# The second mixer's gate projection as seven half-size products, its operand forms written over the activations' own quarters

## The chip, the cores and the metric

The kernel runs on one core of one Trainium2 chip. The metric is the device time of one execution in microseconds (us); lower is better. Five queues of instructions work side by side: TensorE (PE, the matmuls; its weight loads are listed apart as PEld), VectorE (DVE), ScalarE (ACT), GpSimd (POOL, here almost only the issuer of the DMAs that accumulate) and SyncE (SP, the issuer of most other DMAs).

## The reference, cut to what matters

A trunk of two layers on 512 tokens of width 1024, in float32. Layer 0 mixes with gated linear attention (GLA), layer 1 with a gated DeltaNet (GDN); after each comes a gated ConvFFN, and after every sublayer a layer norm. The change lies in layer 1's mixer:

```python
def gdn_mixer(x, w_in, conv_w, a_log, dt_bias, norm_w, w_out):
    proj = x @ w_in
    qkv, gate, beta_lin, a_lin = jnp.split(proj, [...], axis=-1)
    qkv = jax.nn.silu(causal_dwconv(qkv, conv_w))
    ...
    o = rms_norm(gdn_chunked(qc, kc, vc, beta, gc), norm_w)   # the recurrence, 4 chunks
    return (o * jax.nn.silu(gate)) @ w_out
```

The gate is `x` (512 x 1024) times a block of `w_in` (1024 x 1024).

## The kernel before, in words

**Number format.** Every large operand is kept as two float32r parts, a rounded high part and the rest (`xh`, `xl` for the activations, `wh`, `wl` for weights). A product of two such operands takes three matmuls: high by high, high by low, low by high. A weight item is one tile of 128 x 1024 (512 KB): ACT makes the high part by a cast, DVE the low part by a subtraction (`split_out`, line 716).

**Activations.** `xh` and `xl` hold x transposed: eight chunks of 128 features, each over 512 tokens. The quarters of x in what follows are (even or odd chunks) by (first or last 256 tokens): a11 is even and first, a21 even and last, a12 odd and first, a22 odd and last.

**Order of the work.** One Python planner writes all instructions. It takes weight items from `plan`, splits them `look` items ahead of use (`prefetch`), and keeps an estimated clock `clk`. Side work (the recurrence, the conversions) is written as generators, "tasks". After every six large matmuls `pump()` runs each task whose due time has come, as far as its next `yield`; a `yield 2.0` makes it due 2.0 us later on the planner's clock. `wait(name)` runs tasks without writing large matmuls until a flag is set. The program so written is then put in its final order for each engine by a scheduler that may move an instruction that is ready ahead of an earlier one that is not.

**The GDN mixer (`gdn`).** Its 24 head projections go through `fm_items`. Beside them tasks compute a decay, a Gram matrix per head and the inverse of a triangular system (`base`, `inverses`; line 1837 copies the last blocks of a pair of heads into `rm`, after which the flag `("rm", head)` is set). Then `chain(g)` runs the recurrence for heads 4g to 4g+3: four chunks, each of short float32 matmuls named ks, vn, kT, qs, s and o, with a DVE or ACT step between one and the next. Both chains run beside the gate projection.

**The gate projection before.** `gates` calls `x_tm` for each half of the 1024 output columns: 4 blocks of 128 tokens by 8 chunks by 3 matmuls of 128 x 512 (in the profile `tm<-wh,xh`, `tm<-wl,xh`, `tm<-wh,xl`), fed by eight weight items. Each finished block goes through a Silu on ACT (line 1284) into `sg`. `finish(hf)` waits for all four blocks of a half and for the norm of its heads (`r2`), multiplies (line 1972), and `split_y` transposes the result (`yT`) and splits it for the output projection (`out_proj`), whose residual `h` is read back by POOL's DMAs (`unspill`, line 978) and scaled on DVE (lines 987 and 988).

**The same idea elsewhere in this kernel.** The first mixer (`gla`) already computes its v and its gates by `gated`: a product of two 2 x 2 block matrices by seven products of half-size blocks instead of eight. Its forms of x (a11, a22, a12, w1 = a21 - a22, v2 = w1 - a11, v3 = a11 - a21, v4 = v2 + a12) are made by `x_forms` into tiles of their own, as xq (sums), xfh and xfl (parts). Its forms of the weights (`GATED`) are made in place: a tile (`gw`, or `raw`) is split, then another block of weights is added to it by an accumulating DMA on POOL's queue (line 462), then it is split again; one of the sums, t1 = b11 + b12, is made by a load and a DVE addition (line 454). The products accumulate in two pairs of PSUM banks; after each, `update` copies, adds or subtracts (lines 1220, 1228, 1235, 1238).

**Space.** `gdn` opens a pool of 45 slots of 128 x 512, and beside it `tt` and `m2`, two tiles of 128 x 1024 that `base` uses for the 32 x 32 inverses and no longer needs once they are written out (lines 1751 and 1752).

Of the kernel before, what the change touches and what calls it, by code (L numbers as in the profile page):

```python
# [15 lines left out]
P = 128  # L16
D = 1024
S = 512
# [16 lines left out]
GATED_NEW = {"b21": "b21", "b11": "b11", "t1": "b12", "b22": "b22"}  # L35
GATED_IN = {"b21": "b21", "b11": "b11", "t1": "b11", "b22": "b22", "t2": "b11", "t3": "b22", "t4": "b11"}
GATED_SUM = {"t1": "b22", "b22": "b12", "t2": "b21"}
PREPARE = (4.0, 16.0, 48.0, 68.0)
PREPARE_APART = (2.0, 4.5)
LN_EPS = 1e-5  # L40
# [36 lines left out]
class Trunk:  # L77
# [204 lines left out]
    def plan_gated(self, w, col):  # L282
        group = {"w": w, "col": col}
# [154 lines left out]
    def gated_load(self, group, name, i):  # L438


        if name not in GATED_NEW:
            return
        if name == "b11":
            t = self.mp.tile([P, 1024], F32, name=self.uid("gw"), tag="gw", bufs=2)
        else:
            t = self.rp.tile([P, 1024], F32, name=self.uid("raw"), tag="raw")
        self.nc.sync.dma_start(t.rearrange("p (j f) -> p j f", j=2), self.gated_rows(group, GATED_NEW[name], i))
        group[name, i] = t

    def issue_gated(self, group, name, i):  # L450
        nc = self.nc
        t = group[GATED_IN[name], i]
        if name == "t1":
            nc.vector.tensor_add(t, t, group.pop((name, i)))
            self.vec(1.24)
        self.held += 1
        wh = self.wp.tile([P, 1024], F32R, name=self.uid("wh"), tag="wh")
        wl = self.wp.tile([P, 1024], F32R, name=self.uid("wl"), tag="wl")
        self.split_out(wh, wl, t)
        self.vec(1.24)  # L460
        if name in GATED_SUM:
            nc.gpsimd.dma_start(t.rearrange("p (j f) -> p j f", j=2), self.gated_rows(group, GATED_SUM[name], i),
                                accum_op=ALU.add)
        if name in ("b21", "t3", "t4"):
            del group[GATED_IN[name], i]
        return [(wh[:, blk(j, S)], wl[:, blk(j, S)]) for j in range(2)]
# [101 lines left out]
    def tm_half(self, a, n, tail, done, slots=False, pieces=1):  # L568
# [19 lines left out]
        for tb in range(NTB):  # L588
            m = len(ps[tb])
            for piece in range(m):  # L590
# [9 lines left out]
    def x_tm(self, done):  # L600
        a = lambda c, tb: (self.xh[:, c, blk(tb)], self.xl[:, c, blk(tb)])
        self.tm_half(a, NC, 1, done)

    def out_proj(self, a, n, first, final, pieces=1):

# [543 lines left out]
    def x_forms(self, forms):  # L1149


        nc = self.nc
        pair = lambda t: t.rearrange("p (j i) -> p j i", j=2)

        def part(x, odd, tok, k):
            return x[:, 4 * k + odd:4 * k + odd + 3:2, tok:tok + 256]

        def full(odd, tok):
            ts = [self.slot("xq") for _ in range(2)]
            for k, t in enumerate(ts):  # L1160
                nc.vector.tensor_add(pair(t), *(part(x, odd, tok, k) for x in (self.xh, self.xl)))
            return ts

        def split(name, ts):
            forms[name] = []
            for t in ts:
                h, l = self.slot("xfh", F32R), self.slot("xfl", F32R)
                self.split_out(h, l, t)
                forms[name].append((h, l))
            self.set(("form", name), 2.0)  # L1170

        def both(a, b, op, out):
            for x, y, o in zip(a, b, out):
                nc.vector.tensor_tensor(o, x, y, op)

        for tb in range(NTB):
# [24 lines left out]
        split("v3", a)  # L1201

    def gated(self, forms, tag, done, last):


# [2 lines left out]
        top, high, right = ([None, None] for _ in range(3))  # L1208

        def operand(form, c, r):  # L1210
            if form in forms:
                cols = slice(c % 2 * 256 + r * P, c % 2 * 256 + r * P + P)
                return tuple(t[:, cols] for t in forms[form][c // 2])
            chunk = 2 * c + (form != "a11")
            tok = r * P + (256 if form == "a22" else 0)
            return self.xh[:, chunk, tok:tok + P], self.xl[:, chunk, tok:tok + P]
# [28 lines left out]
        for name, form, at in GATED:  # L1245
# [20 lines left out]
            else:  # L1266
                for i in (0, 2):
                    w = self.weight()
                    if name == "t4":
                        self.after = ()  # L1270
                    for r in range(2):
                        terms(i, w, r)
                        self.pump()
                    self.spend()
            if last:
                forms.pop(form, None)
        self.look = LOOKAHEAD

    def gates(self, sg):

        for hf in range(2):
            def done(tb, ps, hf=hf):
                t = self.slot("sg")
                self.nc.scalar.activation(t, ps, AF.Silu)
                sg[tb][hf] = t
                self.set(("sg", tb, hf), 2.0)

            self.x_tm(done)


    def gla_plan(self, w_in, w_out):
# [260 lines left out]
    def gdn_plan(self, w_in, w_out):  # L1552
        for hd in range(DH):
            if hd == HEADSTART:
                self.plan_pad([(w_in, 4096, 8, 0), (w_in, 4104, 8, H0)])
            self.plan_fm(w_in, 1024 + hd * P)
        for base in (2048, 0):
            for hd in range(DH):
                self.plan_fm(w_in, base + hd * P)
        for hf in range(2):  # L1560
            for cp in range(NC // 2):
                self.plan_tm(w_in, 2 * cp * P, 2, 3072 + hf * S)
        self.plan_out(w_out, 0, NC, TAIL)

    def gdn_consts(self, conv_w, a_log, dt_bias, norm_w):
# [24 lines left out]
    def gdn(self, li, g, b):  # L1590
# [370 lines left out]
                                           rr[:, hs4, :], ALU.mult, ALU.mult)  # L1961
            self.set(("r2", g), 2.5)

        def finish(hf):
            for tb in range(NTB):
                yield from self.until(("sg", tb, hf))
            yield from self.until(("r2", hf))
            for tb in range(NTB):
# [100 lines left out]
```

## Time and profile before

| | |
|---|---|
| three timed runs | 1221.22 to 1221.33 us, median 1221.23 |
| the profiled execution | 1221.98 us, its span 1220.2 us |
| PE, DVE, ACT, POOL busy | 99%, 74%, 50%, 13% of the span |
| granted TensorE clock | 1.000 |
| DMA | 149.41 MB, 122 GB/s |
| GDN mixer: head projections from, gate projection from, out projection from | 564.5, 724.7, 820.7 us |

Times in the lines below are us from the span's start; a mean is in ns. Matmuls overlap in the pipeline, so the busy time of one (some 390 ns for 512 columns) is longer than the distance from one to the next; the chain of waits gives the distance, as the length of a piece over its count of matmuls.

### The profile page before, as it was taken

Reading aid. Unit: us, or ns where it says so; the run is one execution under the profiler, and the core shown is the slowest. Engines: PE = TensorE matmul, PEld = TensorE weight load, DVE = VectorE, ACT = ScalarE, POOL = GpSimd, SP = SyncE. Lnnn points to the kernel's source line nnn. Section 1 sums busy time; section 2 is a strip of 40 time slices with the busy share of each in tenths; the row PEclk is TensorE's granted clock in tenths of the full one; section 3 lists DMA queues with packets and bytes.
Section 4 is the critical chain, followed back from the end, with each engine's and each line's share of the span. In section 5 each row is a group of like instructions: output and inputs, shape, how many; then the busy total and the mean of one; then the engine's idle time right before and its main releaser. Section 6 shows DMA issues by size and latency. Waiting matters only on the chain.

```text
span 1220.2 us, 17190 instructions
## 1 busy us (share of the span) xinstructions
PE 1213.6 (99%) x6501; PEld 1025.1 (84%) x6501; DVE 906.1 (74%) x1515; ACT 609.4 (50%) x1072; POOL 160.7 (13%) x203
## 2 busy tenths in 40 slices
PE   9999999999999999999999999999999999999998
PEld 8888888988888888889888888988988888888886
DVE  6989787787757675666789965688687757776667
ACT  5666663544434443454678555544644433443440
POOL 3030101601100110001242030200510100020000
PEclk9999999999999999999999999999999999999999
DMA  8384642536743554433444351335444853383311
GB/s 227 113 164 115 141 154 72 189 105 137 190 122 92 124 95 121 123 102 91 125 125 130 87 136 36 101 107 156 135 125 101 170 178 95 104 171 97 108 65 69
DMA packets 176275, 149.41 MB, mean 122 GB/s; under 512 B 16870, under 2 KB 140842, under 8 KB 176192
## 3 DMA queue, kind: packets, MB, share of 16 engines
q1 hardware_dynamic: 162464, 116.28, 32.2%
q0 software_dynamic: 12768, 31.37, 13.0%
q8 instruction: 51, 0.84, 0.3%
q10 hardware_dynamic: 960, 0.66, 0.2%
q14 instruction: 32, 0.26, 0.1%
HBM read 129.92 MB, written 5.78 MB: 111 GB/s over the span
## 4 chain that ended last, share of the span: by engine, by line
PE 97%; DMA 1%; ACT 1%; DVE 1%; SPq 0%; issue 0%; DVEq 0%
PE fm L213 54%; PE fold L213 19%; PE tm L213 15%; PE o L213 2%; PE xT L231 1%; DMA raw<-in_gla_w_in_dram 1%; PE pq L213 1%; PE pg L213 1%; PE vn L213 1%; PE yT L231 1%; PE V L213 0%; PE ds L213 0%; PE qs L213 0%; PE s L213 0%; PE ks L213 0%; DMA raw<-in_gdn_w_in_dram 0%
## 5 line engine op out<-in xcount | busy, mean ns | idle before, releaser
L213 PE MATMUL fm<-xh,wh 128*128 128x512 f32 (+2 forms) x1096 | 400.4, 368 | 0.7 <-ACT xh L716 0.7
L213 PE MATMUL fm<-xl,wh 128*128 128x512 f32 (+2 forms) x1096 | 398.5, 366 | 0.0
L213 PE MATMUL fm<-xh,wl 128*128 128x512 f32 (+1 forms) x1072 | 391.5, 367 | 0.2 <-DVE wl L716 0.2
L716 DVE TENSOR_TENSOR wl<-raw,wh 128x1024 fp32r<-128x1024 f32 (+1 forms) x158 | 195.4, 1239 | 151.7 <-ACT wh L716 151.3
L716 ACT CAST wh<-raw 128x1024 fp32r<-128x1024 f32 (+1 forms) x159 | 164.9, 1039 | 211.2 <-PE fm L213 135.5
L213 PEld LDWEIGHTS fm<-xh,wh 128*128 128x128 f32 (+1 forms) x1096 | 205.4, 188 | 34.1 <-ACT xh L716 0.9
L213 PEld LDWEIGHTS fm<-xl,wh 128*128 128x128 f32 (+1 forms) x1096 | 205.4, 188 | 32.6
L213 PEld LDWEIGHTS fm<-xh,wl 128*128 128x128 f32 x1072 | 201.2, 189 | 33.7 <-DVE wl L716 0.4
L1019 DVE SCALAR_TENSOR_TENSOR conv<-fm,ffn_cw,conv 128x511 f32<-128x511 f32 x112 | 83.5, 745 | 9.6 <-ACT conv L1017 7.9
L213 PE MATMUL fold<-wh,fh 128*128 128x512 f32 x224 | 87.6, 391 | 0.0
L213 PE MATMUL fold<-wh,fl 128*128 128x512 f32 x224 | 87.2, 389 | 0.0
L213 PE MATMUL fold<-wl,fh 128*128 128x512 f32 x224 | 87.1, 389 | 0.0
L716 ACT CAST wh<-b 128x1024 fp32r<-128x1024 f32 x48 | 50.0, 1054 | 74.2 <-PE fold L213 32.5
L716 DVE TENSOR_TENSOR wl<-b,wh 128x1024 fp32r<-128x1024 f32 x48 | 58.1, 1222 | 22.7 <-ACT wh L716 22.5
L412 POOL DMA_DIRECT2D b<-b x24 | 20.8, 902 | 357.2 <-DVE wl L716 306.7
L1037 ACT ACTIVATE conv<-conv 128x512 f32<-128x512 f32 x44 | 27.8, 632 | 63.3 <-DVE conv L1019 63.3
L1585 DVE SCALAR_TENSOR_TENSOR conv<-fm,gdn_cw,conv 128x511 f32<-128x511 f32 (+2 forms) x72 | 54.0, 788 | 5.1 <-ACT conv L1583 4.6
L213 PEld LDWEIGHTS fold<-wh,fh 128*128 128x128 f32 x224 | 42.0, 188 | 9.6 <-DVE h L1108 1.0
L213 PEld LDWEIGHTS fold<-wh,fl 128*128 128x128 f32 x224 | 42.0, 188 | 8.8
L213 PEld LDWEIGHTS fold<-wl,fh 128*128 128x128 f32 x224 | 42.1, 188 | 8.6
L1019 DVE SCALAR_TENSOR_TENSOR form<-fm,ffn_cw,form 128x511 f32<-128x511 f32 x64 | 47.7, 745 | 1.1
L929 POOL TENSOR_TENSOR h<-h,gb 128x512 f32<-128x512 f32 x16 | 24.1, 1525 | 135.5 <-PE xT L231 134.2
(363 smaller groups left out, 2009.1 us busy)
## 6 DMA issues: line engine op xcount, KB each, us to landing
raw<-in_ffn_w_in_dram SPq DMA_DIRECT2D x88, 512.0 KB, 3.9
raw<-in_gdn_w_in_dram SPq DMA_DIRECT2D x32, 512.0 KB, 4.1
b<-in_ffn_w_out_dram SPq DMA_DIRECT2D x24, 512.0 KB, 6.0
b<-b POOLq DMA_DIRECT2D x24, 512.0 KB, 4.8
raw<-in_ffn_w_out_dram SPq DMA_DIRECT2D x20, 512.0 KB, 3.7
raw<-in_gla_w_in_dram SPq DMA_DIRECT2D x18, 512.0 KB, 4.4
gw<-in_gla_w_in_dram POOLq DMA_DIRECT2D x8, 512.0 KB, 7.5
raw<-in_gla_w_out_dram SPq DMA_DIRECT2D x8, 512.0 KB, 3.7
```

Of the source, the lines that this page charges most:

```text
L213: t = self.nc.tensor.matmul(out, a, b, start=start, stop=stop, skip_group_check=joined)
L231: t = self.nc.tensor.transpose(out, a, self.ident[:n, :n])
L412: self.nc.gpsimd.dma_start(out, group[src, i][:, cols], accum_op=ALU.add)
L716: return self.nc.scalar.copy(dst_h, src), self.nc.vector.tensor_sub(dst_l, src, dst_h)
L929: nc.gpsimd.tensor_mul(h[hf], h[hf], gb[hf])
L1019: nc.vector.scalar_tensor_tensor(a[:, d:], ps[:, :S - d], tap(2 - d), a[:, d:], ALU.mult, ALU.add)
L1037: nc.scalar.activation(a, a, AF.Gelu)
L1585: self.conv = nc.vector.scalar_tensor_tensor(a[:, d:], ps[:, :S - d], tap(3 - d), a[:, d:], ALU.mult, ALU.add)
```

## The change

The gate projection of the second mixer uses `gated`, 7 products of 24 matmuls, in place of `gates` with 192 matmuls. What differs from the first mixer's use of it:

- The forms of x have no tiles of their own for their parts. `x_forms_within` starts when heads 4 and 5 have their inverse, makes w1 from the last 256 tokens and writes its parts over a21's place in `xh` and `xl`; v2 goes over a11 once a11's product is done, v3 over w1 once that is used. v4 is not computed on DVE: v2's sums get the two parts of a12 added by four accumulating DMAs, two for the high part and two for the low part, and v4 is then written over a12.
- b11 lies in `tt` and `m2`, and b12 is added to it by an accumulating DMA as well, without a load and an addition on DVE.
- `finish` works on two blocks of tokens at a time, so a half of the columns is finished in two steps; the Silu is taken by `gate_done` on the combined sums.

```diff
+SPARE = {0: "tt", 2: "m2"}
...
     def gated_load(self, group, name, i):
-        if name not in GATED_NEW:
+        spare = group["spare"]
+        if name not in GATED_NEW or (spare and name == "t1"):
             return
         if name == "b11":
-            t = self.mp.tile([P, 1024], F32, name=self.uid("gw"), tag="gw", bufs=2)
+            t = self.mp.tile([P, 1024], F32, name=self.uid("gw"), tag=SPARE[i] if spare else "gw", bufs=1 if spare else 2)
...
     def issue_gated(self, group, name, i):
-        if name == "t1":
+        if name == "t1" and not group["spare"]:
             nc.vector.tensor_add(t, t, group.pop((name, i)))
...
-        if name in GATED_SUM:
-            nc.gpsimd.dma_start(t.rearrange("p (j f) -> p j f", j=2), self.gated_rows(group, GATED_SUM[name], i),
+        added = "b12" if name == "b11" and group["spare"] else GATED_SUM.get(name)
+        if added:
+            nc.gpsimd.dma_start(t.rearrange("p (j f) -> p j f", j=2), self.gated_rows(group, added, i),
                                 accum_op=ALU.add)
...
+    def x_forms_within(self, forms, part, pair, full, both):
+        nc = self.nc
+        def put(name, ts, odd, tok):
+            for k, t in enumerate(ts):
+                self.split_out(part(self.xh, odd, tok, k), part(self.xl, odd, tok, k), pair(t))
+            forms[name] = (odd, tok)
+            self.set(("form", name), 2.0)
+        yield from self.until(("rm", 5))
+        a = full(0, 256)
+        yield 2.0
+        b = full(1, 256)
+        yield 2.0
+        both(a, b, ALU.subtract, b)
+        yield 2.0
+        put("w1", b, 0, 256)
+        yield 4.0
+        c = full(0, 0)
+        yield 2.0
+        both(c, a, ALU.subtract, a)
+        yield 2.0
+        both(b, c, ALU.subtract, b)
+        c = None
+        yield from self.until(("used", "a11"))
+        put("v2", b, 0, 0)
+        yield 2.0
+        for x in (self.xh, self.xl):
+            for k, t in enumerate(b):
+                nc.gpsimd.dma_start(pair(t), part(x, 1, 0, k).bitcast(F32), accum_op=ALU.add)
+        yield 9.0
+        put("v4", b, 1, 0)
+        b = None
+        yield from self.until(("used", "w1"))
+        put("v3", a, 0, 256)
...
     def gated(self, forms, tag, done, last):
         def operand(form, c, r):
+            if isinstance(forms.get(form), tuple):
+                odd, tok = forms[form]
+                chunk, tok = 2 * c + odd, tok + r * P
+                return self.xh[:, chunk, tok:tok + P], self.xl[:, chunk, tok:tok + P]
...
+            self.set(("used", form))
...
     def gdn_plan(self, w_in, w_out):
-        for hf in range(2):
-            for cp in range(NC // 2):
-                self.plan_tm(w_in, 2 * cp * P, 2, 3072 + hf * S)
+        self.plan_gated(w_in, 3072, True)
...
-        def finish(hf):
-            for tb in range(NTB):
+        def finish(hf, half):
+            blocks = range(2 * half, 2 * half + 2)
+            for tb in blocks:
                 yield from self.until(("sg", tb, hf))
...
-            yield 2.4
-            self.split_y(y, hf, sg, self.gdn_nw, after=None if hf else last)
+            yield 1.6
+            self.split_y(y, hf, sg, self.gdn_nw, blocks, last)
...
         for hf in range(2):
-            self.spawn(finish(hf))
-        self.gates(sg)
+            for half in range(2):
+                self.spawn(finish(hf, half))
+        forms = {"apart": False}
+        self.spawn(self.x_forms(forms))
+        self.gated(forms, "sg", gate_done, True)
         self.wait(("r2", 1))
```

More of the change, by code (lines that the diff above doesn't have):

```diff
@@ L280, in plan_fold, with plan_gated @@
                 self.plan.append(("fold", group, name, quarter, i))
-    def plan_gated(self, w, col):
-        group = {"w": w, "col": col}
+    def plan_gated(self, w, col, spare=False):
+        group = {"w": w, "col": col, "spare": spare}
         for name, _, _ in GATED:
@@ L598, in tm_half @@
                     done(tb, ps[tb][piece], piece, blk(piece, S // m))
-    def x_tm(self, done):
-        a = lambda c, tb: (self.xh[:, c, blk(tb)], self.xl[:, c, blk(tb)])
-        self.tm_half(a, NC, 1, done)
     def out_proj(self, a, n, first, final, pieces=1):
@@ L1174, in both @@
                 nc.vector.tensor_tensor(o, x, y, op)
+        if not forms.get("apart", True):
+            yield from self.x_forms_within(forms, part, pair, full, both)
+            return
         for tb in range(NTB):
@@ L1277, in gated @@
         self.look = LOOKAHEAD
-    def gates(self, sg):
-        for hf in range(2):
[L1282 to L1288, printed above, removed]
     def gla_plan(self, w_in, w_out):
@@ L1559, in gdn_plan @@
                 self.plan_fm(w_in, base + hd * P)
-        for hf in range(2):
-            for cp in range(NC // 2):
-                self.plan_tm(w_in, 2 * cp * P, 2, 3072 + hf * S)
+        self.plan_gated(w_in, 3072, True)
         self.plan_out(w_out, 0, NC, TAIL)
@@ L1962, in chain @@
             self.set(("r2", g), 2.5)
-        def finish(hf):
-            for tb in range(NTB):
+        def finish(hf, half):
+            blocks = range(2 * half, 2 * half + 2)
+            for tb in blocks:
                 yield from self.until(("sg", tb, hf))
             yield from self.until(("r2", hf))
-            for tb in range(NTB):
+            for tb in blocks:
                 t = sg[tb][hf]
@@ L1973, in finish, with gate_done @@
                                                           ALU.mult, ALU.mult)
-            yield 2.4
-            self.split_y(y, hf, sg, self.gdn_nw, after=None if hf else last)
+            yield 1.6
+            self.split_y(y, hf, sg, self.gdn_nw, blocks, last)
+        def gate_done(tb, hf, t, src):
+            nc.scalar.activation(t, src, AF.Silu)
+            sg[tb][hf] = t
+            self.set(("sg", tb, hf), 1.2)
         items = [lambda ps, hd=hd: k_done(ps, hd) for hd in range(DH)]
```

## The prediction

> **What bounds the kernel now.** I read the page first, then the busy time of each engine by stage, then the chain of waits through the gate projection, then the groups of instructions.
>
> ```profile
> PE 1213.6 (99%) x6501; PEld 1025.1 (84%) x6501; DVE 906.1 (74%) x1515; ACT 609.4 (50%) x1072; POOL 160.7 (13%) x203
> ```
> ```profile
> core 0: us, PE busy (x) PEld busy (x) DVE busy (x) ACT busy (x) POOL busy (x), PEclk, DMA share, GB/s
> 59.50:163.50 104.00, 103.93 (x560) 86.81 (x559) 89.48 (x183) 71.46 (x128) 18.16 (x19) 1.00 0.58 129
> 640.00:702.00 62.00, 62.00 (x315) 52.50 (x314) 59.79 (x136) 43.46 (x108) 8.05 (x17) 1.00 0.39 109
> 724.70:748.80 24.10, 24.08 (x343) 20.01 (x342) 15.00 (x41) 11.89 (x42) 0.00 (x0) 1.00 0.24 77
> 748.80:792.80 44.00, 44.00 (x330) 41.28 (x330) 27.73 (x90) 25.57 (x103) 6.42 (x12) 1.00 0.26 79
> 792.80:818.90 26.10, 26.10 (x124) 21.67 (x124) 21.09 (x61) 10.20 (x20) 0.00 (x0) 1.00 0.41 124
> 818.90:861.00 42.10, 42.10 (x203) 35.02 (x201) 36.79 (x67) 21.38 (x40) 5.70 (x4) 1.00 0.40 117
> ```
>
> In each row the length of the stretch stands before PE's busy time. PE has no idle time in the GDN gate projection (the rows from 724.70 to 818.90): this stage is as long as its matmuls, so a matmul taken out is worth its own distance, as long as nothing new is late. DVE is the next engine: 68% busy there (63.8 of 94.2 us). The first two rows are what it has done elsewhere: 86% in the first mixer's two runs of the same scheme, 96% in a stretch of head projections, PE full in both.
>
> **Matmuls.** The three groups of the gate projection, and pieces of the chain of waits (start, length, what):
>
> ```profile
> L213 PE MATMUL tm<-wh,xh 128*128 128x512 f32 x64 | 26.7, 417 | 0.0
> L213 PE MATMUL tm<-wl,xh 128*128 128x512 f32 x64 | 25.1, 393 | 0.0
> L213 PE MATMUL tm<-wh,xl 128*128 128x512 f32 x64 | 25.1, 392 | 0.0
> ```
> ```profile
> 144.13 5.48 PE fold L213 x24
> ...
> 156.18 0.07 issue
> ```
>
> Removed are 3 x 64 = 192 matmuls; added are 7 products x 2 row blocks x 4 chunks x 3 = 168 of the same shape. The 24 fewer are one such piece of the first mixer: 5.48 us. The clock column is 1.00 in every stage, so no gain or loss through it. The 0.07 us of issue is all that the first mixer shows as a gap near the end of its gates.
>
> **Vector and scalar work.** Groups with their mean in ns after the busy time:
>
> ```profile
> L716 DVE TENSOR_TENSOR wl<-raw,wh 128x1024 fp32r<-128x1024 f32 x9 | 11.0, 1221 | 8.3 <-ACT wh L716 8.2
> L716 ACT CAST wh<-raw 128x1024 fp32r<-128x1024 f32 x9 | 9.4, 1050 | 12.6 <-PE tm L213 11.9 <-PE fm L213 0.8
> L1161 DVE TENSOR_TENSOR xq<-xh,xl 128x512 f32<-128x512 f32 x8 | 5.1, 683 | 0.0
> L1174 DVE TENSOR_TENSOR xq<-xq,xq 128x512 f32<-128x512 f32 x8 | 5.2, 684 | 0.1
> L716 DVE TENSOR_TENSOR xfl<-xq,xfh 128x512 fp32r<-128x512 f32 x8 | 5.4, 684 | 0.1
> L716 ACT CAST xfh<-xq 128x512 fp32r<-128x512 f32 x8 | 4.8, 616 | 2.8 <-DVE xq L1174 2.8
> L1220 ACT COPY sg<-fold 128x512 f32<-128x512 f32 x6 | 3.4, 587 | 3.4 <-PE fold L213 3.4
> L1235 DVE TENSOR_TENSOR sg<-sg,fold 128x512 f32<-128x512 f32 x2 | 1.4, 680 | 0.0
> ```
>
> Weight items go from 8 to 14: DVE 6 x 1.221 = 7.3, ACT 6 x 1.050 = 6.3 us. Forms: six sums (4.1), six differences (4.1) and eight low parts (5.5) on DVE, eight casts (4.9) on ACT. Updates: six on DVE (4.1), six copies on ACT (3.5). DVE gets 25.1 us, ACT 14.7. The eight Silus, 32 products with the norm, and the transposes stay in number.
>
> DVE's idle time in the three gate rows is 9.1 + 16.3 + 5.0 = 30.4 us; the stage loses 5.5, so 24.9 are left for 25.1. What overflows goes into the out projection's row, whose residual work is not urgent: over both, (63.8 + 36.8 + 25.1) / (136.3 - 5.5) = 96%, the share of the row from 640 to 702 where PE missed nothing. So DVE's load alone costs nothing in my sum; if that cover is gone it costs what the first rival says. ACT at (47.7 + 14.7) of 88.7 us is 70% and costs nothing.
>
> **Where a form is late.** The order of the products is a12, a11, w1, v4, v2, v3, a22, each 24 matmuls or four groups of six. The first two read x as it is; then w1 is due. From the chain of waits, DVE's timeline, and the matmuls that read `xh`:
>
> ```profile
> 747.20 1.58 PE tm L213 x6
> 748.78 0.89 PE ks L213 x8
> 749.67 0.89 PE vn L213 x8
> 750.56 0.44 PE kT L231 x4
> 751.00 1.39 PE tm L213 x6
> 752.39 0.89 PE vn L213 x8
> ...
> 764.97 1.40 PE tm L213 x6
> ...
> 790.49 1.39 PE tm L213 x6
> ```
> ```profile
> 742.82 0.75 DVE L1837 COPY rm<-R 64x256 f32<-64x256 f32 x2 [3.25 <-PE R L213]
> ...
> 749.71 1.13 DVE L1905 SCALAR_TENSOR_TENSOR yy<-ks,gd_neb,v 128x128 f32<-128x128 f32 x4 [1.73 <-PE ks L213]
> ```
> ```profile
> 724.70:748.80 24.10, 10.71 (x33) 5.22 (x31) 0.00 (x0) 0.00 (x0) 1.00 0.24 77
> ```
>
> Two of every three gate matmuls read `xh`, and 33 by 748.80 (one is a neighbour's) means that 48, a12 and a11, are over there. The forms may start at 743.57, when the third pair of heads has its inverse. Two sums of two and a difference of two, 4.1 us, fit before 749.71, where DVE has little else; the cast and low part of w1 (0.6 + 1.4) come behind the step yy, near 753. Until then PE has the recurrence (2.2 us from 748.78, and as much again behind yy). I take 0.3 us, between 0 and the 1.2 that yy's end (750.84) lies behind ks.
>
> v4 is the tight one. From 748.8 on v2 needs w1's low part, the sum c, two differences and v2's low part, ten operations or 6.8 us of DVE, which is idle 16.3 of 44.0 us there, 0.37 per us: 18.5 us, so v2 is written near 767. Then v4's DMAs:
>
> ```profile
> b<-b POOLq DMA_DIRECT2D x24, 512.0 KB, 4.8
> gw<-in_gla_w_in_dram POOLq DMA_DIRECT2D x8, 512.0 KB, 7.5
> ```
> ```profile
> L978 POOL DMA_DIRECT2D h<-hd x8 | 4.3, 545 | 67.3 <-PE ks L213 67.3
> ```
>
> The low part's DMA adds to the bytes that the high part's has just written, so it waits for that one to land: two after one another of the kind b<-b (4.8 us, from SBUF to SBUF, twice the size) and two issues of 0.5 make 10.7, the writing of v4 2.0: near 780. At the pace of before, w1's four groups end with the one at 764.97, at 766.4. Ten groups stand from 751.00 to 790.49, one every 4.4 us, so from there to 780 three more ran, 4.2 us. They must be replaced by the recurrence, which has 18 us of its own left (26.4 to 792.8, less six groups of 1.4), but whose steps wait for each other, as yy for ks. Bounds are 0 (it fills everything) and 4.2 (it moves no faster than now); I take 1.8, nearer the lower, because two chains cover each other's steps, the short matmuls of one being as long as the vector step of the other.
>
> The Trainium skill (DMA: Bandwidth & Descriptors, "Anatomy of one DMA — SWDGE (gpsimd) path") fits a DMA issued by GpSimd as 2.0 us plus its bytes at 436 GB/s, which for 256 KB is an estimate of 2.6 us. By it v4 would come 4.4 us earlier and the term of 1.8 would be about 1.2. For 512 KB the page's estimate is 3.2 us, where the two accumulating rows here have 4.8 and 7.5, so the sum keeps the rows.
>
> **Edits at nothing.** The weights' sums by DMA: each has two products between its split and the next, 11.0 us at PE's pace, against 7.5 to land and 2.3 to split; without that cover each is a wait of up to 2.3 us. On POOL's queue the new issues stand ahead of the reads of `h`, which have waited 67.3 us for the recurrence anyway. A form's two low-part DMAs wait there for the high parts' landing, with the sums for v3's weights queued behind; those have two products of time. b11 in `tt` and `m2`: the inverses are written out before 712, its split comes after 724. `finish` by halves leaves eight products with the norm behind the last matmul in place of sixteen; PE was not waiting before, so no gain; I put 0.1 at that end after the first mixer's row.
>
> **Sum.** 5.48 - 0.3 - 1.8 - 0.1 = 3.3 us saved. The profiled execution took 1221.98 us, its span 1220.2; after: 1218.7. The median of the runs, 1221.23, is 0.75 below the profiled one: 1217.9.
>
> **Rivals.**
>
> *DVE becomes the bound of the recurrence.* Form and weight operations, which can't be interrupted, stand in front of the chain's steps. Each chain has three yy and three state steps, twelve in all. If half of them lose one operation of 0.68 us without cover, that is 4.1 us on top of the sum's terms, 3.3 - 4.1 = 0.8 lost: 1222.0. If two lose it, 1.9 are saved: 1219.3. For it: not a microsecond of DVE is over in the stage. Against: the row from 640 to 702. Within 0.2% of before either way.
>
> *v4 comes only after w1's product.* The planner lets a task go one step after every six matmuls, some 4.5 us apart here. From w1's writing to v4's DMAs are four such steps, as many as w1's product has groups. If the DMAs are issued there, v4 is 10.7 + 2.0 = 12.7 us off, and the recurrence has five short pieces of 0.89 left: PE stands for 8.2 us. With the 0.4 of the other terms 3.1 us slower than before: 1224.3. It decides from 5.1 us of waiting on. For it: the order of the text. Against: instructions do leave that order when they are ready. In this chain a single gate matmul stands between two halves of a transposition:
>
> ```profile
> 729.64 0.59 PE qT L231 x4
> 730.23 0.24 PE tm L213
> 730.48 0.66 PE qT L231 x4
> ```
>
> *Nothing is late.* The whole 5.48 stays: 1215.8. It is the lower end of the forecast's own case.
>
> **How the numbers follow.** Forecast with PE's new waits from 0 to 3.0 us, 1215.8 to 1218.8: 0.60. First rival (and v4 late by a little), 1218.8 to 1222.2: 0.24. Second rival: 0.16. The range is 1215.6 to 1222.4, which leaves out the second rival; the forecast's own is 1215.8 to 1218.8. A measurement can tell about 0.2%, 2.4 us, from no change: faster 0.60, same 0.24, slower 0.16.
>
> **What would show it.** 168 gate matmuls named fold; PE's idle time in the stage near 2 us, almost all between w1's product and v4's; DVE above 90% there; both accumulating steps of v4 some 5 us each. It is wrong if PE stands more than 3 us at one form, if the recurrence ends later than at 792.8, or if the out projection starts behind 819 (820.7 now).

## The result, and the profile after

| | before | after |
|---|---|---|
| median of the runs | 1221.28 us (1221.22 to 1221.48, 4 runs) | 1235.86 us (1234.63 to 1235.95, 4 runs) |
| profiled execution, its span | 1221.98, 1220.2 us | 1235.88, 1234.2 us |
| granted TensorE clock over the span | 1.000 | 0.993 |

The change makes the kernel slower by 14.6 us: the ratio is 1.0117, with a 95% interval from 1.0099 to 1.0134. The forecast was 3.3 us faster.

The busy times of the page, and then the rows by stage that answer to those of before (columns as in the prediction):

```profile
PE 1216.5 (99%) x6477; PEld 1025.7 (83%) x6477; DVE 929.5 (75%) x1547; ACT 623.4 (51%) x1092; POOL 176.4 (14%) x215
PEclk9999999999999999999999999889999999999999
```
```profile
724.00:744.00 20.00, 18.73 (x285) 14.94 (x285) 15.49 (x38) 12.38 (x34) 4.81 (x4) 1.00 0.72 132
744.00:776.00 32.00, 32.00 (x275) 30.38 (x272) 27.06 (x69) 21.99 (x87) 4.16 (x6) 1.00 0.33 54
776.00:790.00 14.00, 13.16 (x98) 12.03 (x96) 12.29 (x37) 9.89 (x38) 6.45 (x7) 1.00 0.76 152
790.90:797.80 6.90, 5.79 (x14) 4.53 (x15) 4.32 (x10) 3.37 (x11) 2.19 (x4) 0.51 0.64 173
808.10:818.30 10.20, 8.04 (x22) 5.89 (x22) 6.87 (x19) 3.57 (x6) 0.00 (x0) 0.50 0.02 8
724.00:828.00 104.00, 93.26 (x756) 80.40 (x755) 82.03 (x212) 61.68 (x186) 21.19 (x24) 0.92 0.52 112
```

There are the 24 matmuls fewer (6477 for 6501), and TensorE is all the same busy 2.9 us longer (1216.5 for 1213.6). The stage explains it. Of its 104.0 us TensorE stands (has no matmul that may start) for 104.00 - 93.26 = 10.7. And in two stretches, 6.9 and 10.2 us long, the clock column shows 0.5: the 5.79 + 8.04 = 13.8 us of matmuls in them took twice their time, 6.9 us more. Up to 776 only 1.3 us is lost; everything else lies behind the point at which v4 is due. The first head of the next sublayer's projections starts at 874.65 in place of 860.88, 13.8 us later, and from there to the end of the span it is 359.6 us for 359.3: nothing more is lost.

What TensorE waited for, by the view of its waits (us in all, times, longest; the four largest from 724 to 828):

```profile
PE yT L232 <- DVE sg L2005: 4.5, 1, 4.5
PE fold L214 <- ACT xh L715: 2.9, 1, 2.9
PE fold L214 <- DVE sg L1279: 2.2, 1, 2.2
PE vn L214 <- DVE rm L1869: 1.3, 1, 1.3
```

The second row is v4, as feared, but it is not the largest. The first is a transposition of finished gates, which waits for the products with the norm on DVE. The chain of waits tells what stood in front of those (start, length, what):

```profile
797.27 7.47 DMA gw<-in_gdn_w_in_dram
...
804.85 1.05 ACT wh L715
...
805.92 1.23 DVE wl L715
...
807.27 0.36 DVE sg L2005
...
807.68 2.32 PE yT L232 x8
```

A weight item (t4's second) had to be split first, and its sum by DMA was issued only at 797.27. DVE's timeline shows why so late (number of instructions, then in brackets the idle time before and what ended it):

```profile
778.82 0.69 DVE L715 TENSOR_TENSOR xl<-xq,xh 128x512 fp32r<-128x512 f32 x1
...
785.55 1.28 DVE L715 TENSOR_TENSOR xl<-xq,xh 128x512 fp32r<-128x512 f32 x2
...
791.99 0.69 DVE L715 TENSOR_TENSOR xl<-xq,xh 128x512 fp32r<-128x512 f32 x1 [2.80 <-ACT xh L715]
...
794.80 0.69 DVE L715 TENSOR_TENSOR xl<-xq,xh 128x512 fp32r<-128x512 f32 x1 [1.35 <-ACT xh L715]
...
795.50 1.22 DVE L715 TENSOR_TENSOR wl<-gw,wh 128x1024 fp32r<-128x1024 f32 x1
```

These are v2's first low part, v3's two, v4's two, and then the split of t2's second weight item, behind which the last sum is issued. (The profile names an instruction of ACT as what released that sum; but here and in six other runs it is issued 0.55 to 0.57 us after this split ends, whenever that is.) That split needs nothing from v4. It stands behind v4 in DVE's queue, and the queue stands idle for 2.80 and 1.35 us before v4's low parts. So one late form holds a weight, a DMA of 7.5 us, another weight, the products with the norm and the transpositions, one behind the other.

**Theory A**, formed on this: the forms come late, and what they hold up in DVE's queue costs more than the forms themselves; the stands halve TensorE's clock on top. **Rivals**: B, v4's accumulating DMAs alone are too slow; C, the weights' sums by DMA are too slow by themselves; D, the reads of `h` in GpSimd's queue hold up both; E, DVE simply has too much to do; F, the finish by halves puts transpositions too early into TensorE's queue.

### The profile page after: what moved, and what is told of

The parts are those of the page before. It is cut to its first block, busy times and chain, and to the rows that moved or that the text cites. A ratio compares the mean times of both kernels' runs of the same rounds, so it can differ in the third digit from the quotient of the medians.

```text
span 1234.2 us, 17230 instructions
## 1 busy us (share of the span) xinstructions
PE 1216.5 (99%) x6477; PEld 1025.7 (83%) x6477; DVE 929.5 (75%) x1547; ACT 623.4 (51%) x1092; POOL 176.4 (14%) x215
## 4 chain that ended last, share of the span: by engine, by line
PE 93%; issue 2%; DMA 2%; POOL 1%; DVE 1%; ACT 0%; SPq 0%; DVEq 0%; POOLq 0%; ACTq 0%
PE fm L214 53%; PE fold L214 20%; PE tm L214 12%; DMA gw<-in_gdn_w_in_dram 1%; PE o L214 1%; PE xT L232 1%; PE yT L232 1%; PE pg L214 1%; PE ds L214 0%; PE vn L214 0%; PE s L214 0%; PE ks L214 0%; POOL rm L1799 0%; PE warm L797 0%; PE sa L214 0%
## 5 line engine op out<-in xcount | busy, mean ns | idle before, releaser
L715 DVE TENSOR_TENSOR wl<-b,wh 128x1024 fp32r<-128x1024 f32 x48 | 58.4, 1223 | 22.4 <-ACT wh L715 22.0
L214 PE MATMUL fold<-wh,xh 128*128 128x512 f32 x104 | 45.5, 439 | 5.1 <-ACT xh L715 2.9
```

The costliest lines, as they stand in the source:

```text
L214: t = self.nc.tensor.matmul(out, a, b, start=start, stop=stop, skip_group_check=joined)
L715: return self.nc.scalar.copy(dst_h, src), self.nc.vector.tensor_sub(dst_l, src, dst_h)
```

## The experiments

All times are medians. The kernel of before was run again beside each of them and took 1221.2 to 1221.5 us; the two numbers in brackets are the 95% interval of the ratio to it.

**1. Without forms; without sums; without both.** In the first, `x_forms_within` sets the forms to the quarters of x as they are, which leaves out the sums, differences and splits of the forms; in the second the accumulating weight DMAs go:

```diff
-        yield from self.until(("rm", 5))
+        for name, odd, tok in (("w1", 0, 256), ("v2", 0, 0), ("v4", 1, 0), ("v3", 0, 256)):
+            forms[name] = (odd, tok); self.set(("form", name))
+        return
...
-        if added:
+        if added and not group["spare"]:
```

> Leaves out the making of w1, v2, v4 and v3: the seven products take the quarters of x as they lie there. Matmuls, weight items, weight sums, finish by halves stay. Theory A (v4's accumulating steps come late, and DVE's in-order queue holds the split of t2's second weight item behind v4's low parts; the last weight sum, t4's weights and the transposes follow from it, and the granted clock halves in the gaps): nothing late is left, so about 1216 to 1217 us, PE idle in the gate stage under 1.5 us, clock 1.00 throughout. Theory C (the chain of weight sums through GpSimd's queue is too slow by itself): the late last sum stays, 1228 or more. Theory E (DVE has too much to do): in between, since 14 of DVE's 25 us added stay, about 1220 to 1225.

> Leaves out the accumulating DMAs on the second mixer's weights: the products take the weights without the sums. Splits of all 14 weight items stay, and so do the forms. Theory A: v4 stays late (PE stands some 3 us at it, near 789 to 792 us), but t4's weights no longer wait for a DMA, so the stand before the transposes (6.5 us) shrinks; 1221 to 1227 us. Theory B (v4's latency alone costs it all): 1233 or more. Theory C (the weight sums alone): 1216 to 1217.

> Leaves out both the forms of x and the weights' accumulating DMAs; matmuls, splits and finish by halves stay. The price of 24 matmuls fewer with nothing late: 1215.8 us (1221.3 less 5.48). If the finish by halves or the seven-product order by itself costs something, more than 1217.

Measured: without forms 1220.2 us (0.9981 to 1.0003), without sums 1227.2 (1.0032 to 1.0071), without both 1218.0 (0.9963 to 0.9986). Of the 17.8 us between the changed kernel and the last, the forms take 15.7 when they go alone, the sums 8.6; the two make 24.3, more than both together, so they share a loss. B alone and C alone are out: they expected 1233 or more without sums, and 1228 or more without forms. Theory A's 1216 to 1217 without forms was missed by 3 us; part of that is the stand of 7, below. E is not out yet: 1220.2 lies at the lower edge of its 1220 to 1225, for this run also takes the forms' work off DVE. The run without both missed its 1215.8 by 2.2 us.

Without sums, 1227.2 lies just above theory A's range (1221 to 1227), but not for its reason. A expected the stand for v4 to stay and the one at the transpositions to shrink. Nearly the opposite came:

```profile
PE yT L232 <- DVE sg L2005: 3.7, 1, 3.7
PE fold L214 <- DVE sg L1279: 2.2, 1, 2.2
790.00:796.00 6.00, 5.61 (x25) 4.32 (x23) 5.87 (x19) 4.00 (x12) 0.00 (x0) 1.00 0.88 276
796.00:802.00 6.00, 2.31 (x8) 1.20 (x8) 5.59 (x19) 1.72 (x3) 0.00 (x0) 0.91 0.25 93
```

v4 is written at 790.2 in place of 795.5, and TensorE does not stand for it: from v2's writing to v4's it takes 10.7 us in place of 14.2. So the weight sums slowed v4's DMAs. And with no sum to land, the stand at the transpositions is still 3.7 us. From 790 to 802 DVE is busy for 11.5 of 12 us (third busy column): it has the late forms and the weight splits to do one after the other, and the products with the norm stand behind them. So, by these rows, waiting for the last sum accounts for some 0.8 us of the 4.5 at this stand; the rest comes from DVE's queue, which runs late as a whole.

Without both TensorE has no wait left in the stage, and DVE none to give:

```profile
796.00:808.00 12.00, 11.94 (x61) 9.85 (x60) 11.82 (x37) 7.21 (x10) 0.00 (x0) 1.00 0.23 79
808.00:820.00 12.00, 12.00 (x61) 9.96 (x61) 12.00 (x24) 7.46 (x13) 0.00 (x0) 1.00 0.43 127
```

DVE (third busy column) is full from 796 us on, TensorE too, and nothing is lost by it.

**2. v4 on DVE.** Two sums for a12 and two additions in place of the four DMAs:

```diff
-        for x in (self.xh, self.xl):
-            for k, t in enumerate(b):
-                nc.gpsimd.dma_start(pair(t), part(x, 1, 0, k).bitcast(F32), accum_op=ALU.add)
-        yield 9.0
+        c = full(1, 0)
+        yield 2.0
+        both(b, c, ALU.add, b)
```

> v4 is made on DVE (two sums for a12, two additions, 2.7 us of DVE more) in place of the four accumulating DMAs. Theory A: v4's parts are written by about 784 us in place of 795.5, DVE's queue no longer stands before t2's second split, and PE's two stands go or shrink under 3 us together: 1217 to 1222 us, clock 1.00. Theory C: t4's weights stay late, 1229 or more. Theory E (DVE's load): the 2.7 us more of DVE make it worse or leave it, 1234 to 1239.

Measured: 1234.2 us (1.0077 to 1.0136). Theory A as it stood expected 1217 to 1222 and missed; 1234.2 fits C (1229 or more) and E (1234 to 1239). C fell in 1; E is left for 3. DVE's timeline of this run (v2's second low part, a12's sums, the additions, the last of the four low parts of v4 and v3, and t2's second split):

```profile
780.79 0.69 DVE L715 TENSOR_TENSOR xl<-xq,xh 128x512 fp32r<-128x512 f32 x1
...
784.06 1.29 DVE L1160 TENSOR_TENSOR xq<-xh,xl 128x512 f32<-128x512 f32 x2
...
786.90 1.28 DVE L1173 TENSOR_TENSOR xq<-xq,xq 128x512 f32<-128x512 f32 x2
...
793.34 0.68 DVE L715 TENSOR_TENSOR xl<-xq,xh 128x512 fp32r<-128x512 f32 x1
794.11 1.22 DVE L715 TENSOR_TENSOR wl<-gw,wh 128x1024 fp32r<-128x1024 f32 x1
```

Without v4's DMAs the split comes at 794.11 in place of 795.50. The DMAs' latency was not what made the form late: v2 was just as late before it (781.5). So the question became why v2 is late, 14 us behind the forecast.

**3. The pauses.** `x_forms_within` has a `yield` between its steps, and `pump` lets a task go one step after every six large matmuls. Taken out, all but the one behind w1 and the 9.0 us in front of v4 (the diff), or only those behind w1's writing:

```diff
         a = full(0, 256)
-        yield 2.0
         b = full(1, 256)
-        yield 2.0
         both(a, b, ALU.subtract, b)
-        yield 2.0
         put("w1", b, 0, 256)
-        yield 4.0
+        yield 2.0
         c = full(0, 0)
-        yield 2.0
         both(c, a, ALU.subtract, a)
-        yield 2.0
         both(b, c, ALU.subtract, b)
...
         put("v2", b, 0, 0)
-        yield 2.0
```

> The forms start where they did, but the pauses between their steps are taken out: sums, difference and writing of w1 in one go, the rest up to v2's writing in a second. Theory A (pacing): w1's low parts are written near 753 us in place of 761, v2's near 768 in place of 779, the split of t2's second item comes before v4's low parts, and the time is 1218 to 1223 us. Rival (the start at 743 us and DVE's queue set the pace, not the pauses): v2 is still written behind 775 us and the time stays over 1230.

> The changed kernel with the pauses taken out only behind w1's writing (c, the differences, v2, v4's DMAs); w1 is still paced. Theory A counts two pauses of 4.5 us in front of w1's writing and four between w1 and v4's DMAs: about two thirds of the 12.2 us that all pauses cost come back, 1226 to 1229. If what decides is only when w1 begins: 1232 or more.

Measured: 1223.6 us (1.001 to 1.0032) without pauses, 1229.5 (1.0046 to 1.0086) with those in front of w1 left in. The same instructions, 12.2 us less; 6.4 of it by the pauses behind w1, the rest by those before it. Both lie 0.5 to 0.6 us above theory A's ranges (1218 to 1223, 1226 to 1229) and far from the rivals' (over 1230, 1232 or more); A had given the pauses behind w1 two thirds, and they gave half. DVE's timeline without pauses:

```profile
752.99 1.28 DVE L715 TENSOR_TENSOR xl<-xq,xh 128x512 fp32r<-128x512 f32 x2
...
762.20 1.28 DVE L715 TENSOR_TENSOR xl<-xq,xh 128x512 fp32r<-128x512 f32 x2
...
780.29 1.22 DVE L715 TENSOR_TENSOR wl<-gw,wh 128x1024 fp32r<-128x1024 f32 x1
```

w1's low parts start at 752.99 (761.05 with pauses), v2's at 762.20 (778.82), t2's second split at 780.29 (795.50), and the clock is 1.00 throughout. DVE had the room all the time, with the same work to do, so E falls. This is theory A with its first cause found: the forms are paced.

**4. An earlier start, with the pauses kept.** `("rm", 5)` becomes `("rm", 1)`.

> The forms of x start when the first pair of heads has its inverse in place of the third; nothing else differs. Theory A, as it stands after the first four runs (the forms are paced, one step after every six large matmuls, so v2 and v4 land in DVE's queue in front of the split of t2's second weight item, whose sum, t4's weights and the transposes follow): w1 and v2 are written some 10 to 15 us earlier, the split stands in front of v4's low parts, and the time is 1217 to 1222 us with the clock at 1.00. Theory E (DVE has too much to do after the recurrence): the work stays the same, 1230 or more. Against both: the chain of inverses is disturbed and the recurrence itself comes later, over 1225 with PE idle before 760 us.

Measured: 1226.1 us (1.003 to 1.0058), more than the 1217 to 1222 expected: v2 is written by 762 us here too, but TensorE stands 2.6 us in front of 774.4 in the recurrence (`PE o <- ACT vn`). That is the third case, the recurrence disturbed, though not before 760 as it was expected.

**5. The reads of `h` on SyncE's queue** (`nc.gpsimd` becomes `nc.sync` in `unspill`).

> The reads of h and of the layer norm's rows go out on SyncE's queue, not on GpSimd's, where v4's low part and the last weight sum stand behind them. If GpSimd's queue is the cause (theory D): v4's second low-part DMA goes out some 2 to 4 us earlier, and the time falls by 5 us or more, to 1231 or less. If the split of the weights waiting behind the forms in DVE's queue is the cause (theory A): within 2 us of the changed kernel, 1234 to 1237.

Measured: 1236.2 us (1.0094 to 1.0153). No gain: rival D falls. v4's second low-part DMA goes out at 792.12, not earlier than the 790.22 of the changed kernel; it waits for the high part's landing, not for its place in the queue.

**6. The transpositions' place.** First every finish waits for the last product (`yield from self.until(("sg", 3, 1))` in `finish`); then, milder, only the second half's finish is let go 4 us later:

```diff
-            self.set(("r2", g), 2.5)
+            self.set(("r2", g), 6.5 if g else 2.5)
```

> The finish of every half waits until the last product's columns are done, so no transposition stands in TensorE's queue in front of t3's and t4's matmuls; the forms stay as they are. Theory F (the finish by halves puts the transposes too early into TensorE's queue): PE's 6.5 us before the transposes go, 1226 to 1230. Theory A: TensorE waits for t4's weights near 799 us all the same, and the transposes come uncovered at the end; 1234 to 1240.

> The changed kernel with the later finish alone. If the place of the transpositions in TensorE's queue caused the loss by itself: back to 1229 to 1231. By theory A t4's weights stay late (last sum issued near 797, landed near 805 us), so TensorE stands for them in place of the transpositions: 1232 to 1236.

Measured: 1230.9 us (1.0051 to 1.0109) and 1231.5 (1.0063 to 1.01): 5.0 and 4.3 us less, by two executions each. Both theories missed, F by under 1 us: A expected almost no gain, and the stand for v4 (3.0 us in both) and the late weights do stay, but no transposition is waited for any more, and half the clock lasts 3.4 and 6.8 us in all in place of 17.1. So F is a part of the loss.

The kernel of before with its finish cut in halves, nothing else changed:

> The kernel before with one part of the change alone: the finish of a half's columns in two steps of two blocks. The prediction put 0.1 us at the end for it and no gain: 1221.0 to 1221.5. If the steps by halves cost something by themselves (transpositions in front of matmuls in TensorE's queue): 1222.5 or more. If they gain, since fewer products with the norm stand behind the last gate: 1220.5 or less.

Measured: 1221.5 us (0.9991 to 1.001). By itself the cut costs nothing; there the chain has 79 matmuls in one piece between the first transpositions and the next, so nothing of it is urgent.

**7. b12 by a load.** In the kernel without pauses one larger stand was left that all runs share in which b12 is added by a DMA (1.3 to 1.7 us). In the changed kernel's chain:

```profile
732.71 6.53 DMA gw<-in_gdn_w_in_dram
739.27 1.06 ACT wh L715
740.35 1.23 DVE wl L715
741.58 0.10 DVE rs_t L734
741.71 0.43 DVE rm L1869
742.18 0.92 PE vn L214 x4
```

t1's split waits for b12's sum to land, and the copy of an inverse into `rm` stands behind it in DVE's queue, with TensorE waiting. Undone, as in the first mixer, on top of the run without pauses; two more with an earlier start as well, at `("rm", 3)` and `("rm", 1)`:

```diff
-        if name not in GATED_NEW or (spare and name == "t1"):
+        if name not in GATED_NEW:
...
-        if name == "t1" and not group["spare"]:
+        if name == "t1":
...
-        added = "b12" if name == "b11" and group["spare"] else GATED_SUM.get(name)
+        added = GATED_SUM.get(name)
```

> The kernel without pauses (1223.6 us) and besides b12 for t1 loaded into a tile of its own and added on DVE, as in the first mixer, in place of the accumulating DMA. Theory A: in every run with that DMA a weight split waiting for its landing (6.5 us) stands in DVE's queue in front of a copy of the inverse into rm, and TensorE stands 1.3 to 1.5 us near 742 us; the load lands early, the stand goes, DVE has 2.5 us more there where it has room: 1222.0 to 1222.8. Rival (DVE's load): the two additions cost as much as the wait gave, 1223.4 or more.

> As the run before, and the forms start with the second pair of heads' inverse. If what is left over the kernel without forms and sums (1218.0 us) is still lateness of the forms and of the last sum: another 1 to 3 us less, 1219 to 1222. If what is left is DVE's load after the recurrence (full from 796 us on in every run): no change, 1222 to 1223.5.

> As the run before the last, with the start at the first pair's inverse: the forms' 12 sums and differences come before the inverses of the other pairs on DVE. If lateness is what is left: 1219 to 1222. If the forms now delay the inverses and with them the recurrence: 1224 or more, with TensorE standing in front of 760 us.

Measured: 1221.0 us (0.9992 to 1.001), 1223.6 (1.0007 to 1.0026) and 1226.1 (1.0027 to 1.0061). The load gives 2.6 us, more than the 0.8 to 1.6 expected, although DVE has two additions more. An earlier start now costs, where theory A expected 1219 to 1222: TensorE stands 2.3 and 2.7 us near 771 us, waiting for the recurrence's scaling of vn on ACT.

**8. What was left.** On top of the run at 1221.0: the forms' sums and differences on GpSimd; v4 on DVE; the later finish; and the two last together.

> The kernel with no pauses and b12 loaded (1221.0 us), and the twelve sums and differences of the forms on GpSimd in place of DVE: 8.2 us of DVE less; on GpSimd an addition of this shape took 1.55 us in place of 0.69, so w1 and v2 come some 5 us later each. If the 3.0 us that are left over the kernel without forms and sums are DVE's load: 1218.5 to 1220.5, better than before. If they are lateness of the forms: 1222 or more.

> The kernel with no pauses and b12 loaded (1221.0 us), with v4 made on DVE in place of the four accumulating DMAs. If the DMAs' latency of some 11 us still makes something late when the forms are early: 1218 to 1220.5. If not, the 2.7 us more of DVE cost: 1221.3 to 1223.5.

> The kernel with no pauses and b12 loaded (1221.0 us), with the finish of the second half's columns let go 4 us later by the planner, so that the transpositions stand farther back in TensorE's queue. TensorE's stands of 0.65 and 0.25 us before and behind the first transpositions go: 1219.8 to 1220.6. If the transpositions then come uncovered at the end of the gates: 1221.5 or more.

> All four repairs together: no pauses, b12 loaded, v4 on DVE, the finish of the second half's columns let go 4 us later. The two last repairs gave 1.9 and 2.4 us each from 1221.0. If they remove different stands: near 1217. If both only took the same stand before the transpositions: 1218.3 to 1219.2, and the kernel without forms and sums (1218.0) is the floor.

Measured: 1234.3 us (1.0089 to 1.0119) on GpSimd; 1219.1 (0.9971 to 0.999); 1218.6 (0.9968 to 0.9986); both 1219.3 (0.9973 to 0.9991). The run on GpSimd failed by something else (below) and decides nothing about DVE's load. v4 on DVE does: DVE has 2.7 us more to do, and 1.9 us are gained, so its load was not what was left. In the run at 1221.0 TensorE stands 0.7 and 0.2 us at the transpositions and 0.9 in the layer norm behind them; in the next three runs TensorE waits 0 to 0.3 us in that stretch. So the two repairs take the same stands, and together give no more than one (the 1217 for different stands was missed). The version with the later finish beats the kernel of before by 0.2%, some 2.9 us. Its stage:

```profile
724.00:808.40 84.40, 84.29 (x745) 74.23 (x744) 77.34 (x206) 59.07 (x183) 18.53 (x22) 1.00 0.59 131
```

The last gate matmul starts at 808.32 us, in the changed kernel at 827.60, with DVE busy 92% of the stage and TensorE full.

## Why the prediction was wrong, point by point

- **The 24 matmuls, 5.48 us.** Right in kind. With nothing late (without forms and sums) the kernel is 3.2 us faster than before; in the profiled executions the way from the first gate matmul to the next sublayer's first projection is 131.92 us (724.34 to 856.26) for 136.32 (724.56 to 860.88), 4.40 less. So 1.1 us are missing there, 2.3 by the medians. No row of waits shows them, and the idle time of TensorE in that stretch is only 0.2 us more than before; what they are stays open.
- **w1, 0.3 us.** It came near 762, not 753, and still TensorE did not stand: the row from 744 to 776 is full. But the stage paid later: the matmuls of the recurrence ran ahead meanwhile, its last `o` started at 787.47 in place of 791.72, and its cover was gone when v4 was due. (Without pauses it starts at 793.19.)
- **v4, 1.8 us. This step failed.** The prediction put v2 "near 767", from DVE's idle share, 0.37 per us. That DVE had this room is right: without pauses v2 is written at 763.5. But a form's steps don't come when DVE is free. They come when the planner lets the task go, one step per six large matmuls. From the first sum (747.75) to v2's first low part (778.82) that made seven steps of 4.4 us on average, and with them v2 was written at 781.3 and v4 at 795.5, not 780. The prediction had this very mechanism in its second rival, and gave it 0.16 because single matmuls leave the order of the text. It priced it at 8.2 us and one stand, 1224.3; the stand at v4 itself was 2.9, and the time 11.6 us above. The way from v2's writing to v4's was nearly right: 14.2 us for 12.7, and 10.7 without the weight sums; the four DMAs took 3.8 to 7.4 us each, 5.0 in the middle, for 4.8.
- **"Each has two products between its split and the next, 11.0 us". This failed too, and cost most.** The cover was counted from the split, and the split was taken to come on time. It stood behind v4 in DVE's queue, and from there to the split of t4's second weight, with the sum between, it took 805.92 - 795.50 = 10.4 us, when the matmuls that should have covered it had already run. (Without the sums it still took 7.3, with DVE full, so the DMA is the smaller part.) "Without that cover each is a wait of up to 2.3 us" left out what stands behind the waiting split: products with the norm, transpositions and the matmuls behind them, 4.5 + 2.2 us. For t1 it was a copy into `rm`, 1.3 us. The landing (7.5) and the split (2.3) were costed, not what stands behind the split in DVE's queue.
- **"The clock is 1.00 in every stage, so no gain or loss through it."** This failed: it was 1.00 in a kernel whose TensorE hardly ever stood. At two stands, of 2.9 and 4.5 us, the clock went to half for 6.8 and 10.2 us, which is some 6.9 us of the loss.
- **DVE's load at nothing (the first rival).** Right where the forms come early: DVE is full from 796 us on in the best runs, and TensorE is too. With late forms DVE's queue is what TensorE waits for. The sign "DVE above 90%" did not come in the changed kernel (82.03 of 104.0 us, 79%); in its best repair it did (92%).
- **GpSimd's queue and the reads of `h` at nothing; the finish by halves at 0.1.** The first was right (1236.2 without them). The second was right for the kernel of before, and wrong beside late weights: transpositions placed 4 us later gave 4.3 us in the changed kernel and 2.4 in the repaired one.

The account of the 17.3 us between the changed kernel and its best repair, taken in this order: 12.2 for the pauses, 2.6 for b12's sum, 2.4 for the transpositions' place. They overlap: the later transpositions alone gave 4.3. How much of the 12.2 is clock and how much standing the rows show roughly: without pauses the half clock (some 6.9 us) is gone, and TensorE is idle 3.4 us from 724 to 900 in place of 10.7. That makes 14.2, 1.4 more than the two profiled executions lie apart.

Of the prediction's three signs of being wrong only one came, the out projection behind 819 (it starts at 827.99). TensorE stood 2.9 us at a form, not more than 3, and the recurrence ended early: the signs watched the forms, and the larger stand came at a transposition.

## What to carry to other kernels

Cost a late operand by what is queued behind it on every engine in order, not by the wait alone; a split, a copy or a transposition that needs nothing from it may stand there. An engine's idle share says that work fits, not when it is issued: where a planner hands out steps, count its steps from the first release to the due time. And where TensorE has been full, allow in the range for half the clock for 3.4 us or more at a new stand of some 2 us, even though it does not come each time.

## What the runs showed of the hardware

**The clock.** TensorE's granted clock fell to half in steps of one length: in the changed kernel for 6.83 and 10.24 us, in others for 3.41. The rows around the first fall:

```profile
787.50:789.20 1.70, 1.66 (x12) 1.22 (x10) 1.52 (x9) 0.65 (x3) 0.00 (x0) 1.00 1.17 192
789.20:790.50 1.30, 0.00 (x0) 0.00 (x0) 0.00 (x0) 0.00 (x0) 0.28 (x1) 1.00 1.25 198
790.50:791.00 0.50, 0.00 (x0) 0.00 (x0) 0.00 (x0) 0.00 (x0) 0.50 (x2) 1.00 1.19 367
791.00:791.30 0.30, 0.00 (x0) 0.00 (x0) 0.00 (x0) 0.00 (x0) 0.30 (x2) 0.55 1.01 410
```

TensorE had stood for only 1.9 us when the clock was halved (from 789.16, by the busy time in the first row, to 791.03, by the clock in the last). The length of a stand alone does not decide it. Stands of 1.3 to 1.7 us near 742 never did that, and neither did, in the profiled executions, stands of 2.3 (experiment 7, start at `("rm", 3)`), 2.6 (experiment 4) and 3.0 us (experiment 6, first). But one of 2.7 us did (7, start at `("rm", 1)`), and so did two of 1.8 and 1.6 us shortly after one another (3, pauses left in front of w1). The same kernel can go either way: of the six executions of experiment 4 three kept a mean clock of 1.000 and took 1224.2 to 1225.0 us, three had 0.996 to 0.999 and took 1227.3 to 1228.5. The Trainium skill (TensorE: Matmul & The Clock Gate, "Part 1: The HAM clock gate") says that the clock is either full or half, and changes with a free-running window of about 3.4 us. The stretches here, 3.41, 6.83 and 10.24 us at 0.50, agree with it, and so do the two falls in the changed kernel, at 791.03 and 808.09, five times 3.41 us apart. The page gives an idle window as the condition; here the 3.4 us in front of the first fall held some 1.5 us of matmuls, so if that was the window it need not be empty. How full it may be, these runs do not show.

**DVE beside GpSimd.** With the forms' additions on GpSimd, DVE's and GpSimd's timelines:

```profile
744.00 12.94 DVE L1984 TENSOR_TENSOR gd_x<-gd_rr 128x16 f32<-128x16 f32 x2
```
```profile
744.15 5.40 POOL L1161 TENSOR_TENSOR xq<-xh,xl 128x512 f32<-128x512 f32 x4
749.09 2.89 POOL L1175 TENSOR_TENSOR xq<-xq,xq 128x512 f32<-128x512 f32 x2
751.52 2.87 POOL L1161 TENSOR_TENSOR xq<-xh,xl 128x512 f32<-128x512 f32 x2
753.96 2.86 POOL L1175 TENSOR_TENSOR xq<-xq,xq 128x512 f32<-128x512 f32 x2
```

Two products of 128 x 16 on DVE, each with two operands in SBUF, took 12.94 us together, the second 0.16 of it: the first ended when GpSimd's ten sums and differences in a row did, at 756.8. TensorE stood 9.1 us for it, had half the clock for 10.24 us, and the run lost what the repairs had given. (GpSimd does more in this kernel than issue DMAs: before, line 929 alone gives it 16 operations of 128 x 512, 24.1 us.) The Trainium skill (SBUF — State Buffer, "SBUF: two separate sides") has the two engines lock one pair of ports for a whole instruction, and names a VectorE operation with two inputs in SBUF as one that is shut out. The trace agrees, and shows more: one instruction of DVE waited for ten of GpSimd's and got no turn between them. Which of the two came first can't be read from it: the records begin at 744.00 on DVE and at 744.15 on GpSimd, whose times are rough.
